# A block kernel whose projection weights are split into high and low parts once, stored in DRAM, and loaded back as parts in the later token passes

## The chip, the core and the metric

The kernel runs on one core of one Trainium2 chip. The metric is device time in microseconds of one execution. Three executions of the kernel before took 3188.96, 3208.57 and 3228.71 us; their median is 3208.57 us.

The core has a matrix engine (TensorE, PE in the profile; its weight loads stand apart as PEld), three engines for elementwise work (VectorE, DVE; ScalarE, ACT; GpSimd, POOL) and SyncE (SP), which here does little but issue DMAs, in the order of its own instruction list. Each engine works through its list in order. A DMA is carried by the core's 16 DMA engines. Matrices sit in on-chip memory as tiles of 128 partitions.

## What is computed

The reference is one block of a diffusion backbone for 2048 latent tokens and 256 context tokens of width 1024. The part that matters here is the first projection: both token streams are normalised, modulated, and multiplied by `w_in` (1024 x 3328). The first 1792 columns feed a bidirectional RWKV-7 head group, the other 1536 a short convolution.

```
pc = modulate(rmsnorm(ctx, norm1_g[l]), csh1, csc1) @ w_in[l]
px = modulate(rmsnorm(x, norm1_g[l]), sh1, sc1) @ w_in[l]
pc_rw, pc_cv = pc[..., :RWKV_COLS], pc[..., RWKV_COLS:]
px_rw, px_cv = px[..., :RWKV_COLS], px[..., RWKV_COLS:]
...
yx, _, _, rx, kx, vx = rwkv_bidir(xr, xk, xv, xw, xa, w0[l], w_lora_up[l], a0[l], a_lora_up[l],
                                  k_k[l], k_a[l], sf, sb)
...
x = x + g1 * (jnp.concatenate([a_x, b_x], axis=-1) @ w_out[l])
hx = modulate(rmsnorm(x, norm2_g[l]), sh2, sc2)
x = x + g2 * expert_choice_ffn(hx, router_w[l], exp_w_gate[l], exp_w_up[l], exp_w_down[l])
return rmsnorm(x, final_g)
```

All of it is float32. Everything behind the projection (the scan, the output projection, sixteen experts) is untouched by the change.

## The kernel before, in words

**Products in three matmuls.** A float32 operand is split into a high part, rounded to the matrix engine's float32r type, and a low part, the remainder: `split` (L127) casts on ACT (L129) and subtracts on DVE (L134). A product is then high x high, high x low and low x high.

**The projection stage (`proj_phase`, L266).** The 1792 columns are 14 blocks of 128 columns. The tokens are taken in four passes of 512 latent tokens; pass 0 has the 256 context tokens besides. In every pass, for every block, `load_block` (L241) fetches the block's weights in two halves of 128 x 512 float32 (256 KB each) into a staging tile `wr` (two buffers), and splits each half into `wH` and `wL` (three buffers each). So each half is loaded and split four times, once for each pass. `block_mm` (L255) then runs 48 matmuls for the pass's two token tiles of 256: first tile with half 0 (12 matmuls), first tile with half 1, second tile with half 0, second tile with half 1. Its result `pj` is copied out by ACT (L389).

**What follows a block.** The functions in `queue` mix the result with its shifted neighbours (`mixed`, L403) and build the scan's operands: `post_k` (blocks 1 to 4), `post_r` and `post_kd` (blocks 5 to 8), `post_g` (block 9), `post_v` (blocks 10 to 13). `post_kd` is the heaviest: for each of two directions it makes a `ct` and a `bk` tile on DVE, ACT and POOL, and stores them through `to_heads` (L373) to the DRAM tensors C and KBD, 256 and 512 KB each; `post_r` stores NR, 512 KB. Tiles `bk` and `ct` have two buffers.

**The convolution blocks.** The other 12 blocks of `w_in` are loaded and split by the same `load_block` from `conv_gen` (L638), again in four passes, mostly inside the scan stage.

**What sets the order.** The program is written in the order above, and a scheduling layer then orders the instructions of each engine by a simulation of its own (L1654). All loads and stores named here are issued by SP, so they form one list in which an instruction that waits holds all those behind it. A tile's next writer waits until the last reader of that buffer is done.

In this document *a half n* is the n-th half block in program order; its parts go to the buffers that half n-3 used.

Of the kernel before, what the change touches and what calls it, by code (L numbers as in the profile page):

```python
# [7 lines left out]
F32 = mybir.dt.float32  # L8
# [8 lines left out]
D = 1024  # L17
# [3 lines left out]
KT = 8  # L21
# [81 lines left out]
def cvs(k, name, i):  # L103
    a = COLV[name][0] + i
    return k.cv[:, a:a + 1]
# [132 lines left out]
    k.bp = ctx.enter_context(tc.tile_pool(name="sh", bufs=2))  # L238


def load_block(tc, k, I, b):  # L241

    nc = tc.nc
    hs = []
    for half in range(2):
        w = k.bp.tile([128, KT // 2, 128], F32, name="wr", bufs=2)
        nc.sync.dma_start(w, I["w_in"][b][:, half * KT // 2:(half + 1) * KT // 2])
        wH = k.bp.tile([128, KT // 2, 128], F32R, name="wH", bufs=3)
        wL = k.bp.tile([128, KT // 2, 128], F32R, name="wL", bufs=3)
        split(k, nc, wH, wL, w, "act")  # L250
        hs.append((wH, wL))
    return hs

# [12 lines left out]
def proj_phase(ctx_, tc, k, I, S, fill):  # L266
    nc = tc.nc
    bp = k.bp
    with ExitStack() as ctx:
# [320 lines left out]
        for p in range(4):  # L590
            tiles = []
            if p == 0:
                tiles.append(prep_tile(I["ctx"], 0, 1, False, False))
            for q in range(2):
                tiles.append(prep_tile(I["x"], p * 512 + q * 256, 0, p < 3, p > 0))
            if p == 0:
                units = [(0, TC, 0), (TC, 448, 2)]
            elif p < 3:
                units = [(TC + p * 512 - 64, 512, 1)]
            else:  # L600
                units = [(TC + p * 512 - 64, 320, 1), (TC + p * 512 + 256, 256, 6)]
            if p == 0:
                small()
            k.tiles = tiles
            for b in range(14):
                ws = load_block(tc, k, I, b)
                ps = psum.tile([128, 512], F32, name="pj")
                es = []
                if p == 0 and not 5 <= b <= 9:
                    pc = psum.tile([128, 512], F32, name="pc", bufs=1)  # L610
                    block_mm(nc, ws, tiles[:1], [pc[:, :TC]])
                    es.append(evac_ctx(pc[:, :TC]))
                elif p == 0:
                    es.append(None)
                block_mm(nc, ws, tiles[-2:], [ps[:, 0:256], ps[:, 256:512]])
                e = evac_lat(b, p, ps)
                es += [e] * (len(units) - len(es))
                while queue:
                    queue.pop(0)()
                if p == 3 and b >= 12:  # L620
                    fill(1)
                if b == 0:
                    queue.append(lambda u=units, z=es: post_wa(u, z))
                elif b < 5:
                    queue.append(lambda u=units, z=es, j=b - 1: post_k(j, u, z))
                elif b < 9:
                    queue.append(lambda u=units, z=es, j=b - 5: post_r(j, u, z))
                    queue.append(lambda u=units, j=b - 5: post_kd(j, u))
                elif b == 9:
                    queue.append(lambda u=units, z=es: post_g(u, z))  # L630
                else:
                    queue.append(lambda u=units, z=es, j=b - 10: post_v(j, u, z))
# [5 lines left out]
def conv_gen(tc, k, I, S):  # L638

    nc = tc.nc  # L640
    bp = k.bp
    hal = k.cp.tile([128, 4, 3], F32, name="hal")
    nc.gpsimd.memset(hal, 0.0)
    for p in range(3, -1, -1):
        t0 = p * 512
        if p == 3:
            tiles = k.tiles
        else:
            tiles = []
            for q in range(2):  # L650
                hH = bp.tile([128, KT, 256], F32R, name="hH", tag="hH", bufs=2)
                hL = bp.tile([128, KT, 256], F32R, name="hL", tag="hL", bufs=2)
                for half in range(2):
                    r = bp.tile([128, KT // 2, 256], F32, name="hr", tag="xt", bufs=2)
                    nc.sync.dma_start(r, _dap(S["HS"], half * KT // 2 * 128 * T + t0 + q * 256,
                                              [[T, 128], [128 * T, KT // 2], [1, 256]]))
                    ks = slice(half * KT // 2, (half + 1) * KT // 2)
                    split(k, nc, hH[:, ks], hL[:, ks], r, "act")
                tiles.append((hH, hL))
            yield  # L660
        a = 0 if p == 0 else 1
        n = 513 - a - (p == 3)
        for j in range(4):
            cu = bp.tile([128, 515], F32, name="cu", tag="ev", bufs=5)
            b1 = bp.tile([128, 515], F32, name="cb", tag="ev", bufs=5)
            for part in range(3):
                ws = load_block(tc, k, I, 14 + 3 * j + part)
                ps = k.ps()
                block_mm(nc, ws, tiles, [ps[:, 0:256], ps[:, 256:512]])
                if part == 0:  # L670
                    nc.scalar.copy(cu[:, 1:513], ps)
                elif part == 1:
                    nc.gpsimd.tensor_copy(cu[:, 513:515], hal[:, j, 0:2])
                    nc.vector.tensor_tensor(cu[:, 1:513], ps, cu[:, 1:513], op=OP.mult)
                    if p == 0:
                        nc.gpsimd.memset(cu[:, 0:1], 0.0)
                    else:
                        nc.gpsimd.tensor_copy(hal[:, j, 0:2], cu[:, 1:3])
                else:
                    nc.gpsimd.tensor_copy(b1[:, 512:513], hal[:, j, 2:3])  # L680
                    nc.scalar.copy(b1[:, 0:512], ps)
                    if p:
                        nc.gpsimd.tensor_copy(hal[:, j, 2:3], b1[:, 0:1])
                    t = bp.tile([128, 515], F32, name="cvt", tag="ev", bufs=5)
                    nc.scalar.activation(t[:, :n], cu[:, a:a + n], AF.Copy, scale=cvs(k, "cw", j))
                    for q in range(1, 3):
                        nc.vector.scalar_tensor_tensor(t[:, :n], cu[:, a + q:a + q + n], cvs(k, "cw", 4 * q + j), t[:, :n],
                                                       op0=OP.mult, op1=OP.add)
                    nc.gpsimd.tensor_tensor(t[:, :n], b1[:, a:a + n], t[:, :n], op=OP.mult)
                    nc.sync.dma_start(S["CV"][j][:, t0 + a:t0 + a + n], t[:, :n])  # L690
                yield
# [871 lines left out]
def scratch(mk):  # L1563
# [6 lines left out]
    S["C"] = [[S["C_"][d][j] for j in range(4)] for d in range(2)]  # L1570
    for nm in ("TI", "TO"):
        S[nm] = [mk(f"{nm}{n}", [64, 1024], F32) for n in range((NCC + NCL) // 2)]
    S["GR"] = mk("GR", [2, D], F32)
    S["ACC"] = mk("ACC", [T, D], F32)
    S["X1"] = mk("X1", [T, D], F32)
# [82 lines left out]
```

## Time and profile before

| | us |
|---|---|
| median of three executions | 3208.57 |
| the profiled execution, its own time | 3213.07 |
| its span, first to last instruction | 3211.1 |
| projection passes 1 to 3 (read as the stretch 230 to 625 us) | 395 |
| PE busy, share of the span | 90% |
| DVE / ACT / POOL busy | 67% / 43% / 21% |

The profile gives busy times of each engine, the wait that ended last before each instruction, and the share of time in which the DMA engines moved data. PE's busy time has pipelined matmuls in it, which overlap. A row such as `ACT wH L129 <- DMA wr` says that ACT's instruction at line 129 that writes `wH` waited for a DMA that writes `wr`.

### The profile page before, as it was taken

Reading aid. Unit: us, or ns where it says so; the run is one execution under the profiler, and the core shown is the slowest. Engines: PE = TensorE matmul, PEld = TensorE weight load, DVE = VectorE, ACT = ScalarE, POOL = GpSimd, SP = SyncE. Lnnn points to the kernel's source line nnn. Section 1 sums busy time; section 2 is a strip of 40 time slices with the busy share of each in tenths; the row PEclk is TensorE's granted clock in tenths of the full one; section 3 lists DMA queues with packets and bytes.
Section 4 is the critical chain, followed back from the end, with each engine's and each line's share of the span. In section 5 each row is a group of like instructions: output and inputs, shape, how many; then the busy total and the mean of one; then the engine's idle time right before and its main releaser. Section 6 shows DMA issues by size and latency. Waiting matters only on the chain. (4 is left out here: it accounts for less than half of the span.)

```text
span 3211.1 us, 62585 instructions
## 1 busy us (share of the span) xinstructions
PE 2904.7 (90%) x24367; PEld 2629.1 (82%) x24367; DVE 2136.1 (67%) x4611; ACT 1385.1 (43%) x2279; POOL 662.0 (21%) x893
## 2 busy tenths in 40 slices
PE   6878889878999998999999994999999999999997
PEld 4867778768888888877888873989999898999886
DVE  7567766758766666657767746666666666666766
ACT  6446554433344443323454433444444444444443
POOL 0132332443133323212222121001000000001001
PEclk8989899978799999998888986999999999999998
DMA  6355544575556665766566553566666666666786
GB/s 242 122 161 169 196 159 144 177 220 135 137 157 174 158 177 134 222 178 181 140 157 158 122 140 85 168 200 207 220 191 198 192 201 192 208 204 209 262 269 223
DMA packets 407497, 577.43 MB, mean 180 GB/s; under 512 B 174616, under 2 KB 256664, under 8 KB 406176
## 3 DMA queue, kind: packets, MB, share of 16 engines
q1 hardware_dynamic: 396256, 533.58, 54.9%
q0 software_dynamic: 10656, 38.80, 5.3%
q8 instruction: 191, 3.13, 0.4%
q14 instruction: 106, 0.87, 0.1%
q10 hardware_dynamic: 288, 1.05, 0.1%
HBM read 444.73 MB, written 128.59 MB: 179 GB/s over the span
## 5 line engine op out<-in xcount | busy, mean ns | idle before, releaser
L129 ACT CAST wH<-wr 128x1024 fp32r<-128x1024 f32 (+1 forms) x592 | 529.1, 897 | 907.3 <-PE pg L1429 409.4
L134 DVE TENSOR_TENSOR wL<-wr,wH 128x1024 fp32r<-128x1024 f32 (+1 forms) x586 | 625.7, 1072 | 363.4 <-ACT wH L129 358.4
L1429 PE MATMUL pg<-xH,wH 128*128 128x256 f32 x2048 | 587.8, 287 | 18.3 <-ACT s L1433 18.3
L1429 PE MATMUL pg<-xL,wH 128*128 128x256 f32 x2048 | 578.5, 283 | 0.0
L1429 PE MATMUL pg<-xH,wL 128*128 128x256 f32 x2048 | 578.1, 282 | 0.0
L262 PE MATMUL pj<-hH,wH 128*128 128x256 f32 x1600 | 482.1, 302 | 42.8 <-ACT wH L129 22.1
L262 PE MATMUL pj<-hH,wL 128*128 128x256 f32 x1600 | 472.5, 296 | 21.3 <-DVE wL L134 21.2
L262 PE MATMUL pj<-hL,wH 128*128 128x256 f32 x1600 | 471.6, 295 | 1.4 <-DVE hL L134 1.1
L1429 PEld LDWEIGHTS pg<-xH,wH 128*128 128x128 f32 x2048 | 392.1, 192 | 20.4 <-ACT s L1433 19.0
L1429 PEld LDWEIGHTS pg<-xL,wH 128*128 128x128 f32 x2048 | 391.5, 191 | 1.5
L1429 PEld LDWEIGHTS pg<-xH,wL 128*128 128x128 f32 x2048 | 391.9, 191 | 0.0
L262 PEld LDWEIGHTS pj<-hH,wH 128*128 128x128 f32 x1600 | 322.2, 201 | 56.7 <-ACT wH L129 26.3
L262 PEld LDWEIGHTS pj<-hH,wL 128*128 128x128 f32 x1600 | 320.0, 200 | 29.1 <-DVE wL L134 27.0
L262 PEld LDWEIGHTS pj<-hL,wH 128*128 128x128 f32 x1600 | 321.7, 201 | 5.7 <-DVE hL L134 2.0
L1488 POOL DMA_INDIRECT ACC<-o,it x30 | 52.0, 1732 | 968.9 <-DVE o L1474 809.4
L1446 PE MATMUL pd<-wH,hL 128*128 128x512 f32 x512 | 201.9, 394 | 0.0
L1446 PE MATMUL pd<-wL,hH 128*128 128x512 f32 x512 | 201.9, 394 | 0.0
L1446 PE MATMUL pd<-wH,hH 128*128 128x512 f32 x512 | 199.9, 394 | 0.0
L818 DVE TENSOR_TENSOR x<-X,x 128x120 f32<-128x120 f32 (+12 forms) x540 | 157.0, 294 | 58.3 <-DMA X<-TI 46.6
L820 DVE TENSOR_TENSOR X<-X,x 128x120 f32<-128x120 f32 (+12 forms) x540 | 164.8, 308 | 12.3
L782 PE MATMUL pg<-ar,bk 64*128 64x128 f32 x1152 | 136.3, 316 | 21.8 <-DVE g L784 8.1
L782 PEld LDWEIGHTS pg<-ar,bk 64*128 64x128 f32 x1152 | 110.1, 209 | 38.2 <-issue 13.9
(428 smaller groups left out, 5467.1 us busy)
## 6 DMA issues: line engine op xcount, KB each, us to landing
wr<-in_w_gate_dram SPq DMA_DIRECT2D x128, 512.0 KB
wr<-in_w_up_dram SPq DMA_DIRECT2D x128, 512.0 KB
wr<-in_w_down_dram SPq DMA_DIRECT2D x128, 512.0 KB
wr<-in_w_in_dram SPq DMA_DIRECT2D x208, 256.0 KB
bk<-KBD SPq DMA_DIRECT2D x36, 512.0 KB
ar<-NR SPq DMA_DIRECT2D x36, 512.0 KB
adaw<-in_ada_b_dram SPq DMA_DIRECT2D x32, 512.0 KB
inc<-C SPq DMA_DIRECT2D x36, 256.0 KB
```

What stands on the lines that cost most here:

```text
L129: nc.scalar.copy(H_, src)
L134: (leng or nc.vector).tensor_tensor(L_, src, H_.bitcast(F32), op=OP.subtract)
L262: nc.tensor.matmul(ps, wa[:, kw, :], ha[:, kt, :], start=m == 0, stop=m == 3 * KT - 1)
L782: nc.tensor.matmul(pg[:, p], bk[rows, p], ar[rows, p], start=True, stop=True)
L818: nc.vector.tensor_tensor(tv, X[:, 0:r, t:t + 1].to_broadcast([128, r, m]), x[:, t:t + 1, t + 1:].to_broadcast([128, r, m]), op=OP.mult)
L820: nc.vector.tensor_tensor(X[:, 0:r, t + 1:], X[:, 0:r, t + 1:], tv, op=OP.add)
L1429: nc.tensor.matmul(ps, a[:, ws], b[:, kt], start=i == 0, stop=i == 23)
L1446: nc.tensor.matmul(po[2 * m + n], a[:, f, ms], b[:, ns], start=f == 0 and q == 0, stop=f == FB - 1 and q == 2)
L1488: nc.gpsimd.indirect_dma_start(out=S["ACC"], out_offset=bass.IndirectOffsetOnAxis(ap=ids[m][:, :1], axis=0), in_=o, in_offset=None, comput ...
```

## The change

`load_block` is told whether it is the first pass. In pass 0 it loads and splits a half as before, and then stores both parts to new DRAM tensors `WS`, one for each half. In passes 1 to 3 it loads the two parts from `WS` straight into `wH` and `wL`, with no staging tile, cast or subtraction. The convolution blocks load and split as before, and store nothing.

```
-def load_block(tc, k, I, b):
+def load_block(tc, k, I, S, b, first, again=True):
     nc = tc.nc
     hs = []
     for half in range(2):
-        w = k.bp.tile([128, KT // 2, 128], F32, name="wr", bufs=2)
-        nc.sync.dma_start(w, I["w_in"][b][:, half * KT // 2:(half + 1) * KT // 2])
+        ks = slice(half * KT // 2, (half + 1) * KT // 2)
         wH = k.bp.tile([128, KT // 2, 128], F32R, name="wH", bufs=3)
         wL = k.bp.tile([128, KT // 2, 128], F32R, name="wL", bufs=3)
-        split(k, nc, wH, wL, w, "act")
+        parts = [(p, S["WS"][b][half][:, 512 * i:512 * i + 512]) for i, p in
+                 enumerate(w.rearrange("p a b -> p (a b)") for w in (wH, wL)) if b < 14]
+        if first:
+            w = k.bp.tile([128, KT // 2, 128], F32, name="wr", bufs=2)
+            nc.sync.dma_start(w, I["w_in"][b][:, ks])
+            split(k, nc, wH, wL, w, "act")
+            if again:
+                for p, d in parts:
+                    nc.sync.dma_start(d, p.bitcast(F32))
+        else:
+            for p, d in parts:
+                nc.sync.dma_start(p.bitcast(F32), d)
         hs.append((wH, wL))
     return hs
...
-                ws = load_block(tc, k, I, b)
+                ws = load_block(tc, k, I, S, b, p == 0)
...
-                ws = load_block(tc, k, I, 14 + 3 * j + part)
+                ws = load_block(tc, k, I, S, 14 + 3 * j + part, True, False)
...
+    S["WS"] = [[mk(f"WS{b}_{half}", [128, D], F32) for half in range(2)] for b in range(14)]
```

Over the whole program 84 casts leave ACT and 84 subtractions leave DVE (3 passes x 14 blocks x 2 halves). SP issues 140 DMAs more: 56 stores, and 168 loads in place of 84. All of them are 256 KB. PE's instructions are the same in number.

Three places in SP's list show how the scheduling layer places them. The numbers in the names are buffers' serial numbers; line 255 of the changed kernel is the load of the raw half, line 259 the store of a part, line 262 the load of a part.

The first is pass 0, blocks 4 to 6. Before, raw loads follow each other:

```order
L247 DMA wr_1169<-in_w_in_dram 128x512
L247 DMA wr_1277<-in_w_in_dram 128x512
L247 DMA wr_1283<-in_w_in_dram 128x512
L247 DMA wr_1422<-in_w_in_dram 128x512
L247 DMA wr_1428<-in_w_in_dram 128x512
```

and in the changed kernel:

```order
L255 DMA wr_1221<-in_w_in_dram 128x512
L259 DMA WS5_0_114<-wH_1211 128x512
L259 DMA WS5_0_114<-wL_1212 128x512
L255 DMA wr_1331<-in_w_in_dram 128x512
L259 DMA WS5_1_115<-wH_1219 128x512
L259 DMA WS5_1_115<-wL_1220 128x512
L255 DMA wr_1339<-in_w_in_dram 128x512
```

Two stores, each of which waits for its part, now stand ahead of every raw load.

The second is pass 2, blocks 4 to 6, where few other DMAs stand. Before:

```order
L247 DMA wr_4218<-in_w_in_dram 128x512
L561 DMA VB_59<-vb_3981 128x512
L247 DMA wr_4280<-in_w_in_dram 128x512
L247 DMA wr_4286<-in_w_in_dram 128x512
L247 DMA wr_4370<-in_w_in_dram 128x512
```

and in the changed kernel:

```order
L573 DMA VB_59<-vb_4005 128x512
L262 DMA wH_4228<-WS4_1_113 128x512
L262 DMA wL_4229<-WS4_1_113 128x512
L262 DMA wH_4288<-WS5_0_114 128x512
L262 DMA wL_4289<-WS5_0_114 128x512
L262 DMA wH_4292<-WS5_1_115 128x512
L262 DMA wL_4293<-WS5_1_115 128x512
```

Each raw load has become a pair, and each pair goes into the buffers of the third half before it.

The third is pass 2 where the stores of `post_kd` and `post_r` stand (C, KBD and NR). Before:

```order
L247 DMA wr_4693<-in_w_in_dram 128x512
L516 DMA C1_67<-ct_4466 8x16x512
L487 DMA NR_63<-nrb_4141 8x16x1024
L517 DMA KBD0_64<-bk_4439 8x16x1024
L516 DMA C0_66<-ct_4555 8x16x512
L247 DMA wr_4699<-in_w_in_dram 128x512
L517 DMA KBD1_65<-bk_4457 8x16x1024
L247 DMA wr_4811<-in_w_in_dram 128x512
```

and in the changed kernel:

```order
L499 DMA NR_63<-nrb_4157 8x16x1024
L262 DMA wH_4585<-WS8_1_121 128x512
L262 DMA wL_4586<-WS8_1_121 128x512
L262 DMA wH_4685<-WS9_0_122 128x512
L529 DMA KBD1_65<-bk_4457 8x16x1024
L262 DMA wL_4686<-WS9_0_122 128x512
L528 DMA C0_66<-ct_4551 8x16x512
L499 DMA NR_63<-nrb_4157 8x16x1024
L528 DMA C1_67<-ct_4569 8x16x512
L529 DMA KBD0_64<-bk_4542 8x16x1024
L262 DMA wH_4689<-WS9_1_123 128x512
L262 DMA wL_4690<-WS9_1_123 128x512
```

The stores stand in the same list, between the pairs; a low part can have a KBD store ahead of it.

## Rows read from the trace of the kernel before

**Rows 1.** Page, busy time, share of the span and instructions of each engine.

```profile
PE 2904.7 (90%) x24367; PEld 2629.1 (82%) x24367; DVE 2136.1 (67%) x4611; ACT 1385.1 (43%) x2279; POOL 662.0 (21%) x893
```

**Rows 2.** Windows of pass 0: stretch, us, busy time (instructions), granted clock, DMA share, GB/s.

```profile
75.00:140.00 65.00, 60.07 (x468) 57.22 (x468) 33.40 (x54) 34.92 (x63) 6.43 (x31) 1.00 0.32 100
140.00:230.00 90.00, 67.30 (x432) 62.20 (x430) 60.72 (x88) 35.73 (x68) 33.47 (x36) 0.86 0.58 172
```

**Rows 3.** Windows of passes 1 to 3: PE, PEld, DVE, ACT, POOL, clock, DMA share, GB/s.

```profile
230.00:300.00 70.00, 61.42 (x422) 55.23 (x422) 46.95 (x71) 44.52 (x80) 15.14 (x34) 0.91 0.47 154
300.00:365.00 65.00, 49.96 (x273) 44.67 (x273) 48.20 (x61) 30.96 (x55) 29.00 (x26) 0.77 0.65 214
365.00:440.00 75.00, 69.94 (x535) 64.82 (x535) 48.22 (x77) 48.46 (x84) 16.89 (x36) 0.98 0.43 143
440.00:498.00 58.00, 45.61 (x281) 41.66 (x280) 47.78 (x51) 19.11 (x33) 31.89 (x27) 0.85 0.58 199
498.00:570.00 72.00, 67.90 (x535) 65.23 (x534) 50.99 (x91) 40.14 (x76) 12.68 (x38) 1.00 0.42 132
570.00:625.00 55.00, 44.84 (x322) 42.14 (x321) 40.74 (x66) 20.96 (x45) 26.23 (x32) 0.94 0.57 181
```

**Rows 4.** Windows again, line 262 (block matmuls) alone: PE, PEld, clock, DMA, GB/s.

```profile
300.00:365.00 65.00, 39.98 (x222) 37.46 (x222) 0.77 0.65 214
...
440.00:498.00 58.00, 38.45 (x245) 36.55 (x244) 0.85 0.58 199
...
570.00:625.00 55.00, 39.09 (x270) 36.25 (x269) 0.94 0.57 181
230.00:625.00 395.00, 294.40 (x2030) 274.37 (x2030) 0.91 0.52 168
```

**Rows 5.** Lines by form, 230 to 620 us: busy us, mean ns, idle before, releasers.

```profile
L134 DVE TENSOR_TENSOR wL<-wr,wH 128x512 fp32r<-128x512 f32 x81 | 66.9, 833 | 42.3 <-ACT wH L129 40.7 <-PE pj L262 1.3
L129 ACT CAST wH<-wr 128x512 fp32r<-128x512 f32 x82 | 50.1, 618 | 107.9 <-DMA wr<-in_w_in_dram 87.7 <-PE pj L262 19.8
```

**Rows 6.** Waits of PE, 230 to 620 us: us in total, times, longest.

```profile
PE pj L262 <- ACT wH L129: 22.1, 12, 3.4
PE pj L262 <- DVE wL L134: 16.5, 15, 3.0
```

**Rows 7.** Waits of PE, 300 to 365 us.

```profile
PE pj L262 <- ACT wH L129: 12.5, 6, 3.4
```

**Rows 8.** Timeline of PE, 425.2 to 425.8 us: start, duration, instruction.

```profile
425.18 0.28 PE L262 MATMUL pj<-hH,wH 128*128 128x256 f32 x1
425.30 0.28 PE L262 MATMUL pj<-hL,wH 128*128 128x256 f32 x1
```

**Rows 9.** Timeline of SP, three raw loads: start, duration, DMA issued.

```profile
328.73 2.22 SPq L247 DMA_DIRECT2D wr<-in_w_in_dram  x1
...
499.17 0.33 SPq L247 DMA_DIRECT2D wr<-in_w_in_dram  x1
...
586.45 0.97 SPq L247 DMA_DIRECT2D wr<-in_w_in_dram  x1
```

**Rows 10.** Timeline of ACT: the casts of those three halves, idle before and releaser.

```profile
341.84 0.62 ACT L129 CAST wH<-wr 128x512 fp32r<-128x512 f32 x1 [3.17 <-DMA wr<-in_w_in_dram]
...
502.12 0.62 ACT L129 CAST wH<-wr 128x512 fp32r<-128x512 f32 x1 [2.21 <-DMA wr<-in_w_in_dram]
...
593.06 0.62 ACT L129 CAST wH<-wr 128x512 fp32r<-128x512 f32 x1 [3.75 <-DMA wr<-in_w_in_dram]
```

**Rows 11.** Source line 247, 300 to 365 us: issue duration ns min/median/max.

```profile
L247 SPq DMA_DIRECT2D wr<-in_w_in_dram x9: 328/734/2419, 302.7 to 360.7; - x9
```

**Rows 12.** Source line 247, 498 to 570 us.

```profile
L247 SPq DMA_DIRECT2D wr<-in_w_in_dram x19: 327/328/457, 499.2 to 560.9; - x19
```

**Rows 13.** Waits of DVE, 230 to 620 us.

```profile
DVE bk L512 <- DMA KBD<-bk: 19.4, 11, 3.4
```

**Rows 14.** Timeline of ACT, one load of a function table.

```profile
429.91 1.28 ACT L470 ACT_TABLE_LOAD   x1
```

## The prediction

> **What bounds the kernel now.** The page comes first. PE is busy for 90% of the span, DVE for 67%, ACT for 43% [rows 1]. PE is thus the engine to look at, and casts and subtractions lie on engines with room. But these are averages over stages, and the change touches one: the first 625 us.
>
> So the second view is the table of windows over that stage. Passes 1 to 3 fill 230 to 625 us, and they alternate. In the *light* stretches (230 to 300, 365 to 440, 498 to 570 us, 217 us together) PE is busy for 199.3 us and idle for 17.7, and 132 to 154 GB/s move. In the *heavy* ones (300 to 365, 440 to 498, 570 to 625 us, 178 us), where C, KBD and NR are stored, PE is busy for 140.4 us and idle for 37.6, its granted clock is 0.77 to 0.94, DVE is busy for 136.7 us, and 181 to 214 GB/s move [rows 3]. Line 262 has 2030 matmuls in all, 737 of them in the heavy stretches [rows 4]. At 48 a block that is 42.3 blocks, 15.4 heavy and 26.9 light; a heavy block takes 178 / 15.4 = 11.6 us, a light one 217 / 26.9 = 8.1 us.
>
> The third view is who waits for whom. PE waits 22.1 us for casts and 16.5 us for subtractions of weights, 38.6 of its 55.3 us idle [rows 6]; in the worst stretch 12.5 us of 15.0 idle are casts' [rows 3, 7]. Behind that stands the load: ACT was idle for 87.7 us until a raw half landed, and DVE for 40.7 us until a cast was done [rows 5].
>
> The fourth view, the timelines and SP's issues, shows why loads are late. In a light stretch a raw half issued at 499.17 us is cast at 502.12, 2.95 us later; in heavy ones the times are 586.45 to 593.06 (6.6 us) and 328.73 to 341.84 (13.1 us) [rows 9, 10]. Issuing one takes SP 328 ns in the median of a light stretch, but 734 ns and up to 2419 in a heavy one [rows 11, 12]. I read that as a DMA queue that is full and holds SP back. DVE also waits 19.4 us for KBD stores to land before it may reuse `bk` [rows 13]. So the heavy stretches run at the pace of the DMA queue, with DVE close behind; the light ones run at PE's pace.
>
> **The change part by part.**
>
> *Removed:* 84 casts of 0.618 us, 52 us of ACT, and 84 subtractions of 0.833 us, 70 us of DVE [rows 5]. PE's work stays. They reach the end only through PE's waits, at most 38.6 us. If the heavy idle is for weights in the proportion of its worst stretch (12.5 of 15.0), 31 us of the 38.6 are heavy and 7 light.
>
> *Added wait.* Before, a raw half was fetched into `wr` while older halves were still in use, so it could come a block early. Now a pair of loads may start only when PE has finished with the half three before. For the second half of a block that is after matmul 36 of the block before, and it is needed after matmul 12: 24 matmuls. They start 0.12 us apart [rows 8], 2.9 us at full clock. First halves have twice that.
>
> *Light stretches.* The high part needs 2.95 us from its issue, the low part 0.33 more for the second issue, 3.3 us; if its 256 KB also queue behind the first 256 KB at 214 GB/s, 1.2 us more than 2.95, 4.2 us. PE has other work of (199.3 - 176.9) / 26.9 = 0.8 us a block there (176.9 being line 262's 294.4 less its heavy 117.5 [rows 3, 4]); half of it falls into the gap, so 3.3 us are covered. The stall is 0 to 0.9 us a block; I take the middle, 0.5, hence 13 us, less the 7 us of old waits: **+6 us** (ends -7 and +17).
>
> *Heavy stretches.* Each block moves 512 KB more, 8.1 MB in 15.4 blocks. The lower end: the queue has room, and the 31 us of waits go: -31. The upper: all bytes are added at the mean 198 GB/s: +41. Now the stretches move 65 x 214 + 58 x 199 + 55 x 181 = 35.4 MB. If all ran at the best one's rate, 43.5 MB would take 43.5 / 0.214 = 203 us, 25 more than 178. I take **+25 us**, nearer the upper end, because the long issues say that the queue is full. The freed DVE does not help there, since its own buffers wait for the same queue.
>
> A row and a rule part here. The DMA share of 0.57 to 0.65 reads as if a third of the engines' time were free, and by it this term would be 0. The Trainium skill (DMA: Bandwidth & Descriptors, Why a DMA increments its semaphore by 16 and not by 1) says that a transfer is split over the largest number of engines up to 16 that divides both sides' slowest dimension; the stores to C, KBD and NR have 8 there, so eight engines could be full at a share of 0.5, and the term would be an estimated 32.8 KB an engine a block at 20.6 GB/s (214 GB/s over 0.65 x 16 engines), 1.6 us, 25 us in all. No view here tells single engines apart; the long issues speak for the rule.
>
> *Pass 0.* It stores 56 parts, 14.7 MB, each pair ahead of the next raw load in SP's list. Now 75 to 230 us moves 65 x 100 + 90 x 172 = 22.0 MB [rows 2]. The lower end is 0 (shares of 0.32 and 0.58). The upper is 14.7 MB at 214 GB/s on top, 69 us. 36.7 MB at 214 GB/s take 171 us against 155: **+16 us**, near the lower end, because the first 65 us have most of their queue free. A store also holds its buffer; PE holds it longer (36 matmuls, 4.3 us, without the context's 24), so I cost that at nothing. If stores took 13 us as the late load did, it would show as casts waiting for DMAs.
>
> *The rest.* PE's other idle, 55.3 - 38.6 = 16.7 us, is for work of DVE and ACT, which lose a quarter of their load here; I take a third of it: **-5 us**. Four function-table loads come onto ACT, 1.28 us each [rows 14], 5 us beside PE: 0. SP's 84 extra issues in passes 1 to 3 are in the stretches' sums already. Two raw convolution loads move ahead to the end of pass 0; their tile is free in passes 1 to 3: 0.
>
> The sum is 16 + 6 + 25 - 5 = +42 us on the profiled execution's 3213.07: 3255. That execution lies 4.5 us above the median of the runs shown, so I predict **3251 us**.
>
> **The rivals.**
>
> *Weights come in time (17%).* The queue has room, the loads land in 3 us everywhere, the waits of 38.6 us go, with 5 us of the rest, and pass 0 costs 8: -36, 3177, against the median 3173 us. For it: shares of at most 0.65. Against it: 6.6 and 13.1 us landings. The Trainium skill has a fit (DMA: Bandwidth & Descriptors, Anatomy of one DMA — SWDGE (gpsimd) path) of 2.0 us plus the bytes at 436 GB/s, given for GpSimd's DMAs: an estimated 2.6 us for 256 KB, which would favour this rival; the heavy rows disagree with it, the light one is near.
>
> *The second half is late in every block (27%), the slower side.* With no staging tile, the time of a heavy block becomes a loop: two issues 0.66 us, landing, 24 matmuls at the heavy clock of 0.85, 3.4 us, and 0.6 us of other PE work. With the mean of the two heavy landings, 9.9 us, that is 14.6 us against 11.6: 3.0 x 15.4 = +46. The light blocks pay their end, +17, and pass 0 30. That is +93: 3306, or 3302 us. It decides from a heavy landing of 11.6 - 4.7 = 6.9 us on, and one of the two rows is above. The Trainium skill (Trainium Kernel Development and Optimization, Best Practices) asks to double-buffer so that DMA and compute overlap; the change gives up that lead in three passes, and the rule so speaks for this rival. The heavy rows agree with it, the light one does not.
>
> That the change does not do what it says is excluded: the 84 casts and subtractions are gone from the lists.
>
> **How the numbers follow.** The forecast has 56%, and its own range, from half of its heavy and pass-0 terms to one and a half of both, is 3230 to 3275. With the rivals, 8 in 10 lie between 3190 and 3315: below stands most of the first rival, above the part of the second in which landings exceed 10 us. 2% is about what a measurement of this kernel can tell from no change; the bounds are 3144 and 3273. Faster by over 2% needs more than the first rival has: 4%. Slower by over 2% is most of the second rival and the top of the forecast: 24 + 11 = 35%. Within: 61%.
>
> **What would show it.** In the profile after: casts of `wH<-wr` and subtractions fewer by 84; PE's waits in passes 1 to 3 for the DMA of `wH` or `wL`, small in the light stretches (about 0.5 us a block) and large in the heavy ones; the heavy stretches longer by some 25 us at 210 GB/s or more; pass 0 longer by some 16 us, with casts waiting for DMAs; long issue times on SP. I am wrong if the heavy stretches move well over 214 GB/s, if PE hardly waits for the pairs, or if other stages change their length, since the scheduling layer lays out the whole program anew.

## The result, and the profile after

The changed kernel takes 3248.51 us in the median of four executions (3246.84 to 3254.30); the kernel before takes 3207.20 us in four (3188.96 to 3228.71). The ratio is 1.0134, 95% interval 1.0099 to 1.0169: **slower by some 43 us**. The prediction said 3251 us, with a range of 3190 to 3315. The number held, and 1.34% lies within the 2% that had 61%. What was put behind its largest term did not hold, as the experiments show.

The profiled execution took 3249.4 us (span 3247.7), 36 us more than the profiled one before (3213.07). Line numbers have moved by 12: the block matmuls of line 262 are line 274 now, and the loads of the parts stand at line 262.

The page of the kernel after, busy time and instructions of each engine:

```profile
PE 2892.3 (89%) x24367; PEld 2622.0 (81%) x24367; DVE 2087.0 (64%) x4527; ACT 1345.2 (41%) x2199; POOL 645.7 (20%) x893
```

Against [rows 1], DVE has exactly 84 instructions fewer and ACT 80: 84 casts gone, four loads of function tables come. DVE is 49 us less busy and ACT 40, and the kernel is slower all the same. PE's instructions are the same in number, so what PE lost must be idle time or a slower clock; the stage below tells which.

The stage comes next. One mark that is found in every kernel here is the copy-out of a block (ACT, 56 blocks): block 0 of pass 1 is the 15th, block 13 of pass 3 the last. In the timeline of ACT of the kernel after, they are:

```profile
274.70 0.59 ACT L401 COPY e<-pj 128x512 f32<-128x512 f32 x1 [5.63 <-issue]
...
705.06 0.58 ACT L401 COPY e<-pj 128x512 f32<-128x512 f32 x1
```

In the kernel before they started at 250.85 and 648.0 us. So block 0 of pass 1 is out 23.9 us later, and from it to the last block it takes 430.4 us instead of 397.2: 33.2 us more. At the end of the projection the kernel is 57 us behind; of these, 21 us come back in later stages whose code is the same. The mark stands on ACT, which can copy late, so the table of the experiments gives a second length beside it: from the first to the last of PE's 2016 block matmuls of these passes, 399.7 us before and 437.1 us after.

The windows of the kernel after: pass 0 first, then the six stretches of passes 1 to 3, placed as in [rows 3] at where the stores stand (light, heavy, light, heavy, light, heavy), then the whole from mark to mark. Columns as there: PE, PEld, DVE, ACT, POOL, granted clock, DMA share, GB/s.

```profile
75.00:140.00 65.00, 57.03 (x424) 54.16 (x422) 28.75 (x47) 31.36 (x57) 5.33 (x29) 0.95 0.62 204
140.00:275.00 135.00, 92.78 (x551) 83.94 (x552) 77.69 (x121) 57.63 (x108) 34.65 (x48) 0.77 0.64 201
275.00:335.00 60.00, 50.44 (x372) 46.03 (x371) 29.86 (x45) 31.53 (x55) 11.59 (x24) 0.97 0.70 230
335.00:400.00 65.00, 42.61 (x234) 38.35 (x233) 32.64 (x39) 13.89 (x23) 27.07 (x26) 0.79 0.59 197
400.00:470.00 70.00, 65.38 (x508) 62.12 (x507) 31.24 (x53) 35.09 (x58) 13.54 (x34) 0.97 0.62 203
470.00:535.00 65.00, 41.08 (x245) 37.03 (x244) 38.64 (x43) 17.11 (x29) 29.47 (x28) 0.82 0.64 207
535.00:610.00 75.00, 67.56 (x510) 64.38 (x509) 30.82 (x58) 23.16 (x43) 10.12 (x35) 0.93 0.58 187
610.00:665.00 55.00, 40.84 (x247) 37.50 (x246) 34.55 (x56) 20.34 (x41) 18.31 (x28) 0.78 0.58 189
275.00:705.00 430.00, 340.67 (x2339) 316.01 (x2338) 222.82 (x336) 155.05 (x274) 124.20 (x196) 0.89 0.62 201
```

The kernel before, from mark to mark:

```profile
251.00:648.00 397.00, 342.25 (x2381) 316.73 (x2382) 285.59 (x424) 200.50 (x361) 131.93 (x187) 0.92 0.51 166
```

PE is busy for as long as before, 341 against 342 us, at a granted clock of 0.89 against 0.92. What the stage lost is idle time of PE, 89 us where it was 55.

Line 274 alone in the same six stretches:

```profile
275.00:335.00 60.00, 42.81 (x319) 39.85 (x319) 0.97 0.70 230
335.00:400.00 65.00, 33.49 (x194) 32.05 (x193) 0.79 0.59 197
400.00:470.00 70.00, 59.19 (x449) 55.92 (x448) 0.97 0.62 203
470.00:535.00 65.00, 32.33 (x206) 30.78 (x206) 0.82 0.64 207
535.00:610.00 75.00, 64.02 (x468) 60.13 (x469) 0.93 0.58 187
610.00:665.00 55.00, 32.80 (x199) 30.35 (x200) 0.78 0.58 189
```

The light stretches hold 319 + 449 + 468 = 1236 matmuls, 25.75 blocks in 205 us: 8.0 us a block, as before (8.1). The heavy ones hold 599, 12.5 blocks in 185 us: **14.8 us a block instead of 11.6**. And they move 189 to 207 GB/s, no more than before (181 to 214), though every block now has 512 KB more to move. The light stretches move 187 to 230 GB/s instead of 132 to 154 and lose nothing. So rate and loss do not go together: more bytes went through where no time was lost.

Who waited for whom, 275 to 705 us (us in total, times, longest): PE first, then DVE, then SP's list.

```profile
PE pj L274 <- DMA wH<-WS: 54.3, 16, 8.8
PE pj L274 <- DMA wL<-WS: 20.4, 10, 3.8
```

```profile
DVE bk L524 <- DMA KBD<-bk: 46.0, 23, 6.2
```

```profile
SPq L262 <- PE pj L274: 114.6, 53, 8.6
```

PE waits 74.7 us for pairs, where it waited 38.6 us for casts and subtractions [rows 6]: 36 us more, about what the stage lost. By stretch, the 74.7 us are 2.3, 4.0 and 5.2 us in the light stretches, 22.1, 23.6 and 12.8 us in the heavy ones, and 4.6 us behind 665 us. DVE's wait for KBD stores went from 23.5 us in the same stretch of the kernel before to 46.0 ([rows 13] ends earlier and has 19.4):

```profile
DVE bk L512 <- DMA KBD<-bk: 23.5, 15, 3.4
```

SP's line is the new thing in this kernel: SP stands for 114.6 us, in 53 waits, until PE has finished with a buffer into which a pair is to go.

Which pairs are late can be counted, since a block has 48 matmuls and two pairs, and both stand in order. Of the 74.7 us, 68.2 are waits for second halves, which have 24 matmuls of lead, and 6.4 for first halves, which have 48. Of the 20 pairs for which PE waits over 0.3 us, 17 are second halves, among them those of blocks 7 to 11 in passes 1 and 2, all ten. Half of the 20 are issued no later than PE's release of the buffer as the profile has it, and only two more than 2 us behind it: a late pair starts when it may, and lands too late.

One late pair shows how these come together. SP's timeline, then PE's, in pass 1 (start, duration, instruction):

```profile
335.99 0.60 SPq L499 DMA_DIRECT2D NR<-nrb  x1
336.69 2.77 SPq L262 DMA_DIRECT2D wH<-WS  x1
339.56 1.60 SPq L262 DMA_DIRECT2D wL<-WS  x1
```

```profile
335.52 0.28 PE L274 MATMUL pj<-hH,wL 128*128 128x256 f32 x1
335.64 0.28 PE L274 MATMUL pj<-hH,wH 128*128 128x256 f32 x1
...
340.11 0.39 PE L515 MATMUL pw<-xaL,up 128*128 128x512 f32 x1
348.14 0.58 PE L274 MATMUL pj<-hH,wH 128*128 128x256 f32 x1 [7.64 <-DMA wH<-WS]
348.52 0.41 PE L274 MATMUL pj<-hL,wH 128*128 128x256 f32 x1
```

The matmul at 335.52 is the last of block 7 on its first half; with it the buffers come free for the second half of block 8. SP issues that half's pair behind an NR store, at 336.69, some 0.9 us after the release. PE runs the 24 matmuls that are left in between and eight small ones of line 515, and at 340.5 it has nothing to do: the high part has landed at 348.1, 11.4 us after its issue. Behind the wait two matmuls start 0.38 us apart, against 0.12 ahead of it, and the granted clock of this stretch is 0.79, against 0.97 in the light ones on both sides.

The issue times of line 262 (min/median/max ns) in the heavy stretch 336 to 400 us, then in the light one 535 to 610 us:

```profile
L262 SPq DMA_DIRECT2D wH<-WS x8: 325/1078/2773, 336.7 to 386.4; - x8
L262 SPq DMA_DIRECT2D wL<-WS x8: 443/1076/2047, 339.6 to 387.5; - x8
```

```profile
L262 SPq DMA_DIRECT2D wH<-WS x19: 319/320/1423, 538.1 to 608.2; - x19
L262 SPq DMA_DIRECT2D wL<-WS x19: 319/382/852, 538.5 to 609.6; - x19
```

They answer to [rows 11, 12]: 1.08 us in the median where it was 0.73, and 0.32 and 0.38 us in the light stretch, where it was 0.33. That is how the prediction read a full queue. It cannot tell, though, whether the queue's pace or the late start is what PE pays for.

### The profile page after: what moved, and what is told of

Same layout as the page of the kernel before. It is cut to its first block, busy times and chain, and to the rows that moved or that the text cites. A ratio compares the mean times of both kernels' runs of the same rounds, so it can differ in the third digit from the quotient of the medians.

```text
span 3247.7 us, 62639 instructions
## 1 busy us (share of the span) xinstructions
PE 2892.3 (89%) x24367; PEld 2622.0 (81%) x24367; DVE 2087.0 (64%) x4527; ACT 1345.2 (41%) x2199; POOL 645.7 (20%) x893
## 5 line engine op out<-in xcount | busy, mean ns | idle before, releaser
L129 ACT CAST wH<-wr 128x1024 fp32r<-128x1024 f32 (+1 forms) x508 | 478.0, 944 | 785.3 <-PE pg L1441 410.2
L134 DVE TENSOR_TENSOR wL<-wr,wH 128x1024 fp32r<-128x1024 f32 (+1 forms) x502 | 559.1, 1118 | 348.1 <-ACT wH L129 345.3
L274 PEld LDWEIGHTS pj<-hH,wL 128*128 128x128 f32 x1600 | 325.1, 203 | 31.6 <-DMA wL<-WS 26.3
L830 DVE TENSOR_TENSOR x<-X,x 128x120 f32<-128x120 f32 (+9 forms) x540 | 157.8, 294 | 51.0 <-DMA X<-TI 39.0
L832 DVE TENSOR_TENSOR X<-X,x 128x120 f32<-128x120 f32 (+9 forms) x540 | 171.6, 320 | 12.2
```

Of the source, the lines that this page charges most:

```text
L129: nc.scalar.copy(H_, src)
L134: (leng or nc.vector).tensor_tensor(L_, src, H_.bitcast(F32), op=OP.subtract)
L274: nc.tensor.matmul(ps, wa[:, kw, :], ha[:, kt, :], start=m == 0, stop=m == 3 * KT - 1)
L830: nc.vector.tensor_tensor(tv, X[:, 0:r, t:t + 1].to_broadcast([128, r, m]), x[:, t:t + 1, t + 1:].to_broadcast([128, r, m]), op=OP.mult)
L832: nc.vector.tensor_tensor(X[:, 0:r, t + 1:], X[:, 0:r, t + 1:], tv, op=OP.add)
```

## The experiments

**Theory A** is the forecast's: the bytes that were added take their time at a DMA queue that is full. **Theory B** is the mechanism of the second rival: the staging tile gave each load a lead of up to a block, and now a pair starts only when PE releases its buffer; B1 is the form of it in which the harm is SP's list, which stands still behind a waiting pair. Beside these stand the stores of pass 0. Each kernel was timed against the kernel before on the same chip. The stage is the time between the two marks above, and PE the time from its first to its last block matmul of passes 1 to 3, in one profile each (before 397.2 and 399.7 us). The two can differ by 16 us in one run, so small differences of a stage mean little.

| | us | before, us | ratio (95%) | stage, us | PE, us |
|---|---|---|---|---|---|
| the change | 3248.51 | 3207.20 | 1.0134 (1.0099 to 1.0169) | 430.4 | 437.1 |
| e1 stores only | 3207.48 | 3207.27 | 1.0018 (0.9992 to 1.0043) | 403.5 | 396.0 |
| e2 loads only | 3238.18 | 3207.27 | 1.0134 (1.0087 to 1.0182) | 434.5 | 450.5 |
| e3 after, half-major | 3203.54 | 3207.27 | 0.9996 (0.9969 to 1.0024) | 398.1 | 399.7 |
| e4 before, half-major | 3228.12 | 3207.27 | 1.0112 (1.0066 to 1.0159) | 416.9 | 406.9 |
| e5 before + a store | 3221.74 | 3195.10 | 1.0085 (1.0058 to 1.0112) | 429.1 | 433.0 |
| e6 pairs on ACT | 3238.64 | 3195.10 | 1.0139 (1.0090 to 1.0188) | 430.1 | 416.3 |
| e7 hybrid | 3217.90 | 3195.10 | 1.0069 (1.0046 to 1.0093) | 420.8 | 433.6 |
| e8 hybrid, half-major | 3202.86 | 3195.10 | 1.0014 (0.9985 to 1.0043) | 392.0 | 395.2 |
| e9 before + a copy | 3202.29 | 3195.97 | 1.0027 (1.0001 to 1.0052) | 402.2 | 415.7 |
| e10 four buffers | 3212.36 | 3195.97 | 1.0052 (1.0028 to 1.0076) | 405.5 | 404.0 |
| e11 four, half-major | 3214.15 | 3195.97 | 1.0055 (1.0029 to 1.0080) | 391.3 | 381.7 |
| e12 after, half-major | 3198.47 | 3197.55 | 1.0022 (0.9998 to 1.0046) | 394.4 | 395.6 |

### e1 and e2: the change in two parts

In e1 pass 0 stores the parts and the other passes load and split as before. In e2 nothing but one half is stored, and all pairs of passes 1 to 3 come from that one place.

```
 e1:
-        if first:
+        if True:
             ...
-            if again:
+            if first and again:
 e2:
-        parts = [(p, S["WS"][b][half][...]) ...
+        parts = [(p, S["WS"][0][0][...]) ...
             ...
-            if again:
+            if again and b + half == 0:
```

> The changed kernel, but passes 1 to 3 load and split the raw halves as before; the 56 stores of pass 0 stay and nobody reads them. In the traces block 0 of pass 1 is copied out 24 us later after the change than before (274.7 against 250.9 us). Theory of two costs (stores in pass 0, loads in passes 1 to 3): 20 to 30 us slower than before, about 3230 us, all of it gained before block 0 of pass 1. Rival (the loss comes from the loads alone, and pass 0 is longer because pass 1's first pairs stand in its list): within 8 us of before, about 3210 us.

> The changed kernel without its pass 0 stores except those of the first half block: all later passes load that one pair of parts for every half, so the weights of passes 1 to 3 are wrong, but as many bytes move by as many loads. Theory of two costs: pass 0 as before, passes 1 to 3 some 33 us longer as in the trace after the change: 3225 to 3240 us. Rival (stores alone cost, and delay everything behind them): about 3207 us. If the two costs share a cause, this and the run with stores alone add up to more than the change's 41 us.

The stores by themselves cost 6 us, somewhere between -3 and +14: the 20 to 30 us that were expected of them are out, though in e1's profile block 0 of pass 1 is out 16.8 us late, as in the kernel after. What pass 0 loses in that profile does not show in the median of ten executions. The loads by themselves cost all that the change costs, 1.34%. So the cause stands in passes 1 to 3.

### e3 and e4: more time between release and use

The matmuls of a block are put half by half: both token tiles with half 0, then both with half 1. A buffer then comes free after 24 matmuls of its half, and every pair has 48 matmuls of lead, where second halves had 24. No byte is added or taken. e4 does the same to the kernel before. (In e3 and e4 both tiles raise a start flag in the same bank, and part of the first tile's sum is lost; the instructions and their order are whole. e12 mends that.)

```
-    for (hH, hL), ps in zip(tiles, outs):
-        m = 0
-        for kt in range(KT):
+    m = [0] * len(outs)
+    for kh, (wH, wL) in enumerate(ws):
+        for q, ((hH, hL), ps) in enumerate(zip(tiles, outs)):
+            for kw in range(KT // 2):
             ...
```

> The changed kernel with the block matmuls in another order: both token tiles with half 0, then both with half 1. Now 48 matmuls (5.8 us) lie between the release of a buffer and its next use, in place of 24, with the same bytes, the same loads and the same buffers. Theory A of the prediction (the heavy stretches run at the DMA queue's pace, and 8 MB are added to them): passes 1 to 3 stay some 30 us longer than before, total 3240 to 3250 us. Theory B (a pair may start only when PE releases the buffer, so its landing time is exposed, and SP's wait for PE holds the stores behind it): PE's waits for the pairs fall from 75 us to under 40, total 3205 to 3225 us.

> The kernel before with the same other order of block matmuls. Theory A: the queue's pace is unchanged, within 10 us of before. Theory B: before, raw halves already come a block early, so only part of the 38.6 us of weight waits goes: 0 to 20 us faster, 3187 to 3207 us. If it gains as much as the changed kernel does from this order, the order helps by itself and does not tell the theories apart.

e3 loses nothing against the kernel before: the whole 1.3% is gone, with all the stores and loads in place. That speaks for B and against A. One sign of B missed: PE's waits for pairs fall to 59.9 us, not under 40.

e4 missed: the order was expected to be a gain for the kernel before, too, or nothing, and it costs 1.12%. In its trace the time goes at the starts of passes (block 0 of pass 2 is out 17.1 us late, of pass 3 29.5 us): from the last copy-out of a pass to the first of the next it takes 31.6 and 26.3 us, where the kernel before has 7.6 and 4.7. In the first of these gaps stand 21 of PE's transposes of the next pass's tokens, of which the kernel before has one there:

```profile
L360 PE MATMUL pt<-ident,xt x21: 270/418/475, 374.6 to 404.0; 128*128 128x128 f32 x21
```

In the second stand 17, where the kernel before has none, and e3 has none in either. Inside the passes, from block 0 to block 13, the order gains 8 to 9 us a pass in the kernel before (122.0, 113.7 and 123.3 us against 129.9, 122.9 and 132.2). So e4's loss goes with where the scheduling layer put the preparation of tokens, and the order is worth something in itself: e3's gain is not all lead of the pairs.

### e5: the same bytes as stores

The kernel before, and in passes 1 to 3 a 256 KB store of every `wH` half: as many bytes as the change adds there.

```
         split(k, nc, wH, wL, w, "act")
+        if again:
+            nc.sync.dma_start(S["WS"][b][half], wH....bitcast(F32))
```

> The kernel before, which loads and splits raw halves in every pass, with one 256 KB store of the high part for each half in passes 1 to 3, to a DRAM tensor nobody reads: the same 22 MB more as the changed kernel moves in these passes, but the early load into the staging tile stays. Theory A (bytes at the queue's pace): 25 to 40 us slower, 3232 to 3247 us. Theory B (a pair may start only when PE releases the buffer, so the landing is exposed): within 12 us of before, 3200 to 3220 us.

It costs 0.85%, 27 us, and by the numbers that is A's 25 to 40 us. But the experiment has two things in it: the store also keeps `wH`'s buffer until it has landed, and it stands in SP's list until the cast is done. Its trace has both: PE waits 33.0 us for casts and 26.9 for subtractions, together 21 more than before [rows 6], and SP stands 68.8 us in front of the stores for casts. So e5 does not decide, and e9 was made to part the two.

### e6: SP's list

The pairs are issued from ACT's list, so that no store and no other load stands behind a pair that waits.

```
-                nc.sync.dma_start(p.bitcast(F32), d)
+                nc.scalar.dma_start(p.bitcast(F32), d)
```

> The changed kernel with the pairs' loads issued from ACT's list in place of SP's, so that their wait for PE's release no longer holds the stores of C, KBD and NR behind it on SP. Theory B1 (SP's wait holds the stores, which hold DVE's buffers): passes 1 to 3 get back 15 us or more, 3210 to 3235 us, unless ACT's own work behind its waits is as late. Theory B2 (the pair's own landing after the release is what costs): no gain, 3240 us or more; theory A says the same.

The ratio is 1.0139 and the stage by the copy-outs 430.1 us, as with SP. But the copy-outs are ACT's, and ACT now stands at the pairs' waits; on PE the stage is 416.3 us, 21 shorter than with SP. PE's waits, 270 to 700 us:

```profile
PE pj L274 <- DMA wH<-WS: 25.1, 11, 4.4
PE pj L274 <- DMA wL<-WS: 18.2, 15, 5.3
PE pw L515 <- ACT sg L518: 13.8, 7, 3.6
PE pw L515 <- ACT a L522: 9.1, 4, 4.1
```

The waits for pairs fall from 74.7 to 43.3 us, and those for ACT's own `sg` and `a` rise from 1.7 to 22.9. So e6 moves a cost from SP's list to ACT's, as its expectation allowed, and leaves B1 open by itself. Other readings speak against B1 as the main cost: a late pair of the changed kernel is mostly issued at the release, and DVE still waits for KBD stores in e10 and e12 below, which win most of the stage or all of it back (there 42.3 and 41.6 us, where the changed kernel has 46.0).

### e7 and e8: staging kept in the heavy blocks

Blocks 6 to 11 are loaded raw and split in every pass, as before; the other eight go the new way. e8 has the half-major order besides.

```
-                ws = load_block(tc, k, I, S, b, p == 0)
+                ws = load_block(tc, k, I, S, b, p == 0 or 6 <= b <= 11, not 6 <= b <= 11)
```

> The changed kernel in which only blocks 0 to 5, 12 and 13 are stored and loaded back as parts; blocks 6 to 11, whose halves are used while C, KBD and NR are stored, load and split raw halves in all four passes. In the trace after the change the heavy blocks went from 11.6 to 13.9 us and the light ones from 8.1 to 7.7. If the loss is the heavy blocks' (theories A and B): 3195 to 3215 us. Rival (the loss is at the pass boundaries or in the light blocks): still 3230 us or more.

> The kernel of the run before (blocks 6 to 11 raw) with the half-major order of the block matmuls, its accumulation flags set for two groups in one bank. If the lead of a pair is what counts in the light blocks too: 5 to 20 us below that run, 3180 to 3205 us. If the order costs at the pass boundaries as it did in the kernel before: the same or slower than that run.

e7 has 0.69%, half of the loss, and lies above what was expected. (The 13.9 and 7.7 us a block in its expectation are not what the windows above give, 14.8 and 8.0.) In its stage PE still waits 32.5 us for pairs, and 24.0 for casts and subtractions: some late pairs belong to the other eight blocks. Since both bytes and staging change, it agrees with either theory. e8 is again level with the kernel before.

### e9: the bytes alone

The kernel before, and behind each raw load of passes 1 to 3 a copy of the same 256 KB from DRAM to DRAM: 84 copies, 22 MB, as much as the change adds there. The copy holds no buffer, and nothing waits for it. (It writes no on-chip memory, which a load does.)

```
         ...
+        ld = nc.sync.dma_start(w, src).ins
+        if extra:
+            with tc.issue_after(ld):
+                nc.sync.dma_start(S["WX"][extra - 1][b][half], src....)
```

> The kernel before, with one 256 KB copy from DRAM to DRAM behind each raw load of passes 1 to 3, on the same queue: the same extra 22 MB in the same places, but no tile is held and nothing waits for the copies; the early load into the staging tile stays. Theory A (the heavy stretches run at the queue's pace and the bytes lengthen them): 25 to 40 us slower. Theory B (the lead that a half has over its use is what counts; a store of the high part, tried before, also holds that part's buffer): within 10 us of before.

It costs 0.27% (0.01 to 0.52), 9 us; the 25 to 40 us of A lie outside. In its one profile the stage is 5 us longer by the copy-outs and 16 us by PE. The window from mark to mark of e9, two stretches in which it stores KBD and NR, and PE's waits from mark to mark:

```profile
258.00:660.00 402.00, 336.15 (x2347) 309.80 (x2348) 275.57 (x422) 201.63 (x361) 128.99 (x187) 0.92 0.65 214
303.00:370.00 67.00, 46.26 (x281) 40.35 (x279) 45.55 (x60) 33.20 (x56) 29.81 (x28) 0.82 0.67 217
445.00:501.00 56.00, 39.28 (x234) 34.83 (x234) 40.20 (x47) 19.15 (x33) 26.08 (x27) 0.85 0.66 225
```

```profile
PE pj L266 <- ACT wH L129: 27.3, 14, 5.0
PE pj L266 <- DVE wL L134: 15.8, 14, 3.3
```

Over 402 us, light and heavy together, 214 GB/s go through: the rate that the prediction took for the best stretch's limit is here the mean of the stage, more than the changed kernel's 201, and two heavy stretches move 217 and 225 GB/s. PE waits 43.1 us, 4.5 more than before [rows 6]. **Theory A falls**, as far as copies stand for loads: the queue carries as many bytes more. What counts is when a load may start.

### e10 and e11: the lead alone

The changed kernel, with every fourth pair of passes 1 to 3 in the two buffers of `wr`, which it no longer needs there. A pair then goes into the buffers of the fourth half before it, with 60 matmuls of lead by the count that gives 24 with three. The bytes are the same. e11 has the half-major order besides.

```
+        k.nh = 0 if first else getattr(k, "nh", 0) + 1
+        tags = [("wH", 3), ("wL", 3)] if k.nh % 4 else [("wr", 2), ("wr", 2)]
         ...
```

> The changed kernel in which every fourth pair of passes 1 to 3 goes into the two staging buffers, which stand empty there: four halves rotate in place of three, in the same memory, with the same loads. A pair may now start when the half four before is released, 60 matmuls (7.2 us) ahead of its use for both halves of a block. Theory A: no change, 3235 us or more where before is at 3205. Theory B: 25 us or more are won back, at most 10 us slower than before.

> The run before (four halves rotate) with the half-major order of the block matmuls and flags set for two groups in one bank. A pair then has 72 matmuls. Theory A: no change against the changed kernel. Theory B: lead above the landing time wins nothing more, so within 10 us of the run with four buffers; as the order cost the kernel before 36 us by itself, it may also be slower.

e10 has 0.52% where the change has 1.34%: the fourth buffer wins back 0.82%, 26 us (the two intervals taken together leave some 14 us each way). Its window and PE's waits:

```profile
274.00:679.00 405.00, 338.51 (x2393) 319.36 (x2392) 228.74 (x338) 158.38 (x277) 129.09 (x195) 0.90 0.65 214
```

```profile
PE pj L278 <- DMA wH<-WS: 40.0, 12, 7.0
PE pj L278 <- DMA wL<-WS: 9.2, 5, 3.9
```

The stage is 25 us shorter than the changed kernel's, and PE's waits for pairs fall from 74.7 to 49.2 us, by the same 25 us, while the rate rises from 201 to 214 GB/s. Same bytes, less time. The waits for second halves fall from 68.2 to 19.5 us. What is left has another cause: of the 15 late pairs half are issued 6.7 us or more after the release, behind other entries of SP's list. So with more lead SP's list does become a cost.

By its total e11 adds nothing to that, and at 0.55% (0.29 to 0.80) it lies above e3 (-0.31 to 0.24); by theory B more lead should not have made it worse. Its profile has the loss elsewhere: the stage is 14 us shorter than e10's (22 us on PE) and PE's waits for pairs are 38.1 us, but from there to the last `wy` matmul of the scan it takes 1278 us against 1235, at a granted clock of 0.90 against 0.92.

### e12: the half-major order once more

As e3, with one start and one stop flag for both tiles, so that nothing is left out.

```
-    ... start=m == 0, stop=m == 3 * KT - 1)
+    ... start=q == 0 and kt + i == 0, stop=q == n - 1 and kt == KT - 1 and i == 2, ...)
```

> The half-major order of the changed kernel once more, three buffers, now with one start flag for the two groups of a bank, so that both groups' sums are kept (the run before set a start flag for each group, by which part of the first group's sum was lost). Same instructions, bytes and order. Theory B: as that run, within 10 us of before and 30 us or more below the changed kernel. Rival (that run's time came from its layout or from the flags): 15 us or more slower than before, as the run with four buffers and this order was.

The ratio is 1.0022 (0.9998 to 1.0046), 36 us better than the change as it was made. The profiled execution, 3174.05 us, is the quickest of its twelve, so the trace shows this kernel at its best. The window and the waits:

```profile
269.00:664.00 395.00, 331.71 (x2374) 311.79 (x2373) 228.09 (x335) 160.45 (x278) 127.54 (x196) 0.93 0.66 219
```

```profile
PE pj L274 <- DMA wH<-WS: 37.2, 14, 6.6
PE pj L274 <- DMA wL<-WS: 19.5, 5, 8.2
```

395 us and 219 GB/s: with this order the stage can be as short as it was before. Not all of that is lead: PE's waits for pairs are 56.7 us, 18 less than in the changed kernel, of the 36 us that the stage won; PE is also busy for 9 us less, at a granted clock of 0.93 against 0.89. No version beats the kernel before; with this order, the change is worth nothing that these runs can tell.

## Why the prediction was right, and where it was not

**The total.** That it came out within 3 us is in part luck. In the profile pass 0 is 24 us longer where 16 was said, passes 1 to 3 are 33 us longer where 6 and 25 were said, and later stages give back 21 us where -5 was said: +36 between the two profiled executions. That other stages change their length was named as a sign of being wrong, and it came.

**What was removed.** As said: 84 casts and 84 subtractions, which reached PE only through its waits for them, 38.6 us [rows 6]. Those are gone, and 74.7 us of waits for pairs stand in their place. The kernel got slower with two engines less busy.

**Light stretches, +6.** The mechanism held: PE waits 11.5 us for pairs in 25.75 blocks, 0.45 us a block where 0.5 was taken. The blocks take 8.0 us instead of 8.1, so the term is nearer to -3, inside its ends of -7 and +17.

**Heavy stretches, +25.** This is the step that failed, in its reason. "All bytes are added" at a queue that is full would need 210 GB/s or more in these stretches, as the prediction's own list says; they moved 189 to 207. The same bytes without a hold on buffers cost 9 us (e9). The kernel before itself moves 243 GB/s from 0 to 80 us and 270 from 3040 to 3120 us, though with other transfers, so 214 was no limit that its trace showed. In place of it stands the second rival's mechanism: a pair cannot start before PE's release, its landing took 11.4 us in the pair shown, and 24 matmuls do not cover that. The rival's heavy block was worked out as 14.6 us, and 14.8 us is what it takes. That is close by luck, too: not every second half is late, but 17 of 42, and the landing of 9.9 us came from two rows, of which the 13.1 us is the longest of the 21 raw halves that ACT waited for in the heavy stretches (median 6.6). Where the rival's sum went wrong is in the rest: it let the light blocks pay 17 us and pass 0 30, and it counted 15.4 heavy blocks, where 12.5 lie in the heavy stretches now. (One of the 15.4 is a convolution block, 48 matmuls that write `pc` in 570 to 625 us, and gets no pair.) The stage lost 33.2 us; the forecast's two terms for it are 31, the rival's 63. So the size was right and the cause was not, and the long issue times, on which the choice rested, fit both. (One slip in the sums: one and a half of the two terms gives +62.5 us, so the forecast's own range ends at 3271, not 3275.)

**The two rules.** The Trainium skill (Trainium Kernel Development and Optimization, Best Practices) asks for double-buffering so that DMA and compute overlap. The runs agree, and give it a measure for this kernel: with one more buffer 26 us come back, with the other order of matmuls 36, not all of them by lead. The rule on how a transfer is split (the Trainium skill, DMA: Bandwidth & Descriptors, Why a DMA increments its semaphore by 16 and not by 1) was given the long issue times as its support. No view here tells single engines apart, and e9 shows that the size which came out by it, 25 us, is not what the bytes cost.

**Pass 0, +16.** In the profile block 0 of pass 1 is 23.9 us late; in the whole time, e1 puts the stores at 6 us. The sign that the prediction named is missing: casts wait 18.8 us for raw loads from 75 to 275 us, and in the kernel before 31.9 us from 75 to 230. What else holds pass 0 was not settled.

**The rest, -5.** No run takes it apart from the others. Later stages differ between profiles by up to some 20 us with the same code in them: the expert stage, from its first to its last gate matmul, takes 1169.3 us in the profile before, 1156.6 in the one after and 1146.9 in e12's. A single profile can place a loss inside the projection; its total it cannot.

**The account.** Of the 43 us, lead lost is some 26 (e10 against the change), bytes 9 (e9) and stores 6 (e1). The sum is 41, but each has an uncertainty of 8 to 14 us, and the parts need not add: e2, without the stores, costs as much as the whole.

**What stays open.** Why the scheduling layer puts the preparation of tokens at the pass boundaries in e4 and, at one of them, in e11, and not in e3 and e12; why e11's scan takes longer; what SP's list costs by itself. The layer lays out the whole program anew for every edit, and effects of half a per cent may come from that alone; no run here tells.

## What to carry to other kernels

A load straight into an operand's buffer may start only when that buffer is released, so a staging tile that is taken away takes lead with it: compare the work between release and reuse with the landing time in the busiest stretch, not with the mean one, and for each use by itself (here it was the second halves). A queue with long issue times is not yet a queue without room: add the same bytes with nothing waiting for them, and see (e9's copies took SP up to 2.9 us to issue, too). Before work is moved from engines with room to DMAs, look for one more buffer or another order of the consumer.

## What was not expected of the hardware

In the changed kernel, a 256 KB high part for which PE waited was used 3.0 to 5.3 us after its issue in the light stretches and up to 12.2 us after it in the heavy ones, though both move much the same bytes (187 to 230 and 189 to 207 GB/s): the mean rate does not tell how long one load takes to land. And 22 MB more through the queues of a stage of 400 us, from 168 GB/s [rows 4] to 214, cost only 9 us when nothing waited for them.
